# A decoder step whose second MLP block returns to eight products, with a chain for the final squares and later sums and loads

## The chip, the core and the metric

One core of one Trainium2 chip runs the whole step in one launch. The metric is device time in microseconds, the median of the runs shown.

## What is computed

One decoder layer over a prompt of 2048 tokens and a sample of 8 x 4 tokens: a mixer (state-space and retention groups in parallel), attention over 256 memory tokens, an MLP with squared ReLU, and a final norm. The change lies in the MLP and the norm behind it:

```
h = rmsnorm(x, p['g_mlp'])
x = x + jnp.square(jax.nn.relu(h @ p['w_up'])) @ p['w_down']
...
y_prompt = rmsnorm(xp, g_final)
y_sample = rmsnorm(xs, g_final)
```

with a model width of 1024 (eight tiles of 128 features, `KT`) and a hidden width of 4096.

## The kernel before

Features lie on the partitions, tokens in the columns. The prompt is cut into four blocks of 512 tokens, `blk[0]` to `blk[3]`. After the mixer, each block goes through the output projection (`out_items`), attention, and the MLP (`mlp_items`), one block after another. Block 1 carries the 32 sample tokens: their attention is done by 48 small "sample units" (`sample_items`), each with a 512 KB weight of its own, which are put between the units of block 1's MLP; their columns then join block 2, whose MLP works on 544 columns in two pieces of 272.

Numbers are fp32, and the products get their accuracy from splits: a tile is written as a high part (ACT, rounded to the matmul's format) and a low part (the rest, by DVE or POOL), and a product is three matmuls (`PASSES`). So each weight unit of 128 x 1024 numbers is loaded into `raw` (three buffers), split into `whl` (three buffers), and used by PE. The loader works a few units ahead. All loads and stores of this part are issued from one queue, SP, in order: one that waits holds up those behind it.

The MLP runs in eight groups `g` of 512 hidden features. The order is up(0), up(1), down(0), up(2), down(1), ..., up(7), down(6), down(7).

- **Direct down** (`down_items`, block 0): four units of 24 matmuls of 512 columns; each output tile is added to `x` by DVE. PSUM tiles are called `dn`, and the hidden operands `actl`.
- **Seven products** (`up_seven`, `hidden`, `down_seven`, `seven`; blocks 1 to 3): the weight, the hidden tensor and the result are cut in quarters, and seven products of half the columns take the place of eight (`JOBS`). POOL squares the ReLU into `hc`, forms sums and differences of quarters, and each of seven operands is split into `actl`. PSUM tiles are called `m` here; each of the 14 jobs of a group ends with two half-width additions into `x` on DVE. Seven units of weights per group.
- The weight's own sums and differences of quarters (`sums`) are made once, by a side program that starts with block 0: it loads half of `w_s[n]` into `wsum`, POOL makes four operations, and the result is stored to `s_d`; 32 halves in all. `seven_src` reads `w_s` or `s_d`.

The instructions of every engine are put in order when the program is built. `Order` follows a model of the engines' times; side programs (generators) are resumed when the model's clock passes their wake time, and a `yield` of a number, or of a key of the table `SET`, adds that many nanoseconds before the next step. So `SET["ws1"]` and `SET["ws2"]` say how far apart the steps of `sums` stand. `cat_load` is the side program that loads the next block's eight mixer tiles (`cat_d`) and splits them into `act`; it starts, with six loads of the next block's `xT`, when up(7) is done. `squares` makes the sum of squares (`acc`) for a norm: ACT squares a tile into a `relu` buffer (two of them), POOL or DVE adds it. In `seven` it was called in the last group, right behind the last job of each half.

Line 200 is the helper that records every operation of DVE, ACT, POOL and SP, and line 454 the one for matmuls; so tiles, not lines, tell instructions apart.

Of the kernel before, what the change touches and what calls it, by code (L numbers as in the profile page):

```python
# [13 lines left out]
AF = mybir.ActivationFunctionType  # L14
ALU = mybir.AluOpType
# [3 lines left out]
P = 128  # L19
# [7 lines left out]
SB = 1  # L27
TM_ = BT + NS
KT = D // P
# [30 lines left out]
    "l_ds": 4, "x_hs": 2, "x_hq": 2, "x_hl": 2, "q_h": 250, "ws": 700, "ws1": 1500, "ws2": 5000}  # L60


class Item:
# [268 lines left out]
def tile_decoder_step(ctx: ExitStack, tc: tile.TileContext, ins: dict, outs: dict):  # L332
    nc = tc.nc
    model = Model()
    V, A, G, SY = (Engine(model, e, k) for e, k in ((nc.vector, "V"), (nc.scalar, "A"), (nc.gpsimd, "G"), (nc.sync, "SP")))
    T = nc.tensor

    def E(key):
        return Either(model, (V, G), key)
# [59 lines left out]
    def aux(name="ax"):  # L399
        return psum.tile([P, 512], F32, tag="ra", name=name, bufs=2)  # L400
# [7 lines left out]
    def xin():  # L408
        return com.tile([P, TM_], F32, tag="x", name="x", bufs=3)

    def act():
        return com.tile([P, 2, TM_], F32R, tag="act", name="act", bufs=NA)
# [29 lines left out]
    od = Order(model, load_unit, split_unit)  # L442
# [27 lines left out]
    def split(dst, src, scale=None):  # L470

        split_first(dst, src, scale)
        split_rest(dst, src, scale)
# [405 lines left out]
    def pt(name, shape, tag, bufs=1, dt=F32):  # L879
        return pool[name].tile(list(shape), dt, tag=tag, name=tag, bufs=bufs)  # L880

    def call(f):
        return Item(f)
# [145 lines left out]
    def shared_acc():  # L1029
        return com.tile([P, TM_], F32, tag="acc", name="acc")  # L1030
# [673 lines left out]
    def rk(shape, tag, bufs=1, dt=F32):  # L1704
        return pt("rest", shape, tag, bufs, dt)
# [4 lines left out]
    def squares(B, o, t, lo=0):  # L1710
        x, c = B["x"][o], slice(lo, t)
        if o == 0:
            if lo == 0:
                B["acc"] = shared_acc()
            A.activation(B["acc"][:, c], x[:, c], AF.Square)
        elif lo:
            if o > 1:
                V.tensor_tensor(out=B["acc"][:, c], in0=B["acc"][:, c], in1=B["sq"][:, c], op=ALU.add)
            B["sq"] = rk((P, TM_), "relu", 2)
            A.activation(B["sq"][:, c], x[:, c], AF.Square)  # L1720
        else:
            sq = rk((P, TM_), "relu", 2) if "rest" in pool else xin()
            A.activation(sq[:, c], x[:, c], AF.Square)
            (V if "tail" in B else E("x_rq")).tensor_tensor(out=B["acc"][:, c], in0=B["acc"][:, c], in1=sq[:, c], op=ALU.add)
# [27 lines left out]
    def cat_load(B):  # L1752
        t, c0 = B["t"], B["c0"]
        B["cats"], cs = [], []

        def dma():
            ci = xin()
            SY.dma_start(ci[:, :t], cat_d[len(cs), :, c0:c0 + t])
            cs.append(ci)
        dma()  # L1760
        dma()
        for k in range(KT):
            if k == NA - 4 and B["b"] == 0:
                while "hold" in M:
                    yield 500
            yield [cs[k]]
            if k + 2 < KT:
                dma()
            a = act()
            split(a[:, :, :t], cs[k][:, :t])  # L1770
            B["cats"].append(a)
# [339 lines left out]
    def mlp_items(B, nxt):  # L2111
        t = B["tm"]
# [117 lines left out]
        def seven(g, u, name, st):  # L2230
            h = t // 2

            def job(w):
                v = w.rearrange("p s (k m c) -> p s k m c", k=2, m=2)
                while name not in a_of[g]:
                    od.resume(hid[g])
                for m in range(2):
                    if name in ("A11", "S1"):
                        st[name, m] = (aux2 if name == "S1" and not held["zps"] else dense)("m7")
                    ps = st["S1" if name in ("S1", "S4") else "A11", m] if name != "A12" else aux("m7")  # L2240
                    for k in range(2):
                        for i, (a, b) in enumerate(PASSES):
                            mm(ps[:, :h], v[:, a, k, m, :], a_of[g][name][:, k, b, :h],
                               start=(name in ("A11", "A12", "S1") and k + i == 0), stop=(k == 1 and i == 2), skip_group_check=True)
                        yield
                    o = 4 * u + m + (2 if name in ("A22", "S1", "S3") else 0)
                    lo = h if name in ("S2", "S4", "S1", "S3") else 0
                    V.tensor_tensor(out=B["x"][o][:, lo:lo + h], in0=ps[:, :h], in1=B["x"][o][:, lo:lo + h], op=ALU.add)
                    if name == "A22" and g == 7:
                        if B["last"] and u:  # L2250
                            B["tail"] = True
                        squares(B, o - 2, t)
                        squares(B, o, t)
                B["prog"] = 14 * g + 7 * u + JOBS.index(name) + 1
            return job

        def down_seven(g):
            jobs = []
            for u in range(2):
                st = {}  # L2260
                for name in JOBS:
                    src = {"A11": ("w", 0), "A22": ("w", 1), "A12": ("w", 3), "S2": ("s", 0), "S1": ("s", 1),
                           "S3": ("s", 2), "S4": ("s", 3)}[name]
                    jobs.append((seven(g, u, name, st), src + (2 * g + u,)))
            for a, b in zip(jobs[0::2], jobs[1::2]):
                def fn(hl, a=a, b=b):
                    for i, j in enumerate((a, b)):
                        yield from j[0](hl[:, :, 512 * i:512 * i + 512])
                yield Item(fn, seven_src(a[1], b[1]), "v2", tag="l_ds")
            if g == 7:  # L2270
                yield call(lambda: B.__setitem__("fin", od.spawn(final(B, 0, t), B["acc"])))

        def mixed(items, part=1.0):
            for n, i in enumerate(items):
# [8 lines left out]
        count, smp = [0], sample_items()  # L2283
        yield call(lambda: B.__setitem__("ms", od.spawn(mlp_scale(), B["acc"])))
        hid = {}
        B["prog"] = 0
        use = [B["b"] > 0] * 8
        yield from (up_seven if use[0] else up_items)(0)
        yield Item(None, side=lambda: B["ms"])
        for g in range(8):  # L2290
# [44 lines left out]
    def final(B, lo, hi):  # L2335
        n, c, more, x = hi - lo, slice(lo, min(hi, BT)), hi > BT, B["x"]
        end = B["last"] and hi == BT
        cols = [(B["acc"][:, i:i + P], P) + ((B["sq"][:, i:i + P],) if lo else ())
                for i in range(lo, min(hi, BT), P)]
        if more:  # L2340
            cols.append((B["acc"][:, BT:hi], NS))
        if not end:
            yield SET["fi0"]
        rs = stats(pool["rest"], B["acc"], cols, "nf")
        if end:
            for o in (2, 5, 7):
                A.activation(x[o][:, lo:hi], x[o][:, lo:hi], AF.Copy, scale=g_fin[:, o:o + 1])
        else:
            yield "fi1"
        rf = rk((P, TM_), "rb")  # L2350
        ps = yield from spread(rf, rs, n, 4, rk((P, TM_), "sq") if n >= BT else None)
        if not end:
            yield "fi2"
        for i, o in enumerate((0, 2, 1, 3, 5, 4, 6, 7) if end else range(KT)):
            xo = x[o][:, lo:hi]
            if end:
                if o in (2, 5, 7):
                    G.tensor_tensor(out=xo, in0=xo, in1=rf[:, :n], op=ALU.mult)
                else:
                    V.scalar_tensor_tensor(out=xo, in0=xo, scalar=g_fin[:, o:o + 1], in1=ps[:, :n],  # L2360
                                           op0=ALU.mult, op1=ALU.mult)
            elif o % 3 == 2 or B["last"] and o % 3 == 1:
                A.activation(xo, xo, AF.Copy, scale=g_fin[:, o:o + 1])
                G.tensor_tensor(out=xo, in0=xo, in1=rf[:, :n], op=ALU.mult)
            else:
                V.scalar_tensor_tensor(out=xo, in0=xo, scalar=g_fin[:, o:o + 1], in1=rf[:, :n],
                                       op0=ALU.mult, op1=ALU.mult)
            (A if end and i % 2 else SY).dma_start(outs["yT"][o, :, B["b"] * BT + lo:B["b"] * BT + c.stop], x[o][:, c])
            if more:
                SY.dma_start(outs["yT"][o, :, SEQ:], x[o][:, BT:hi])  # L2370
            if not end:
                yield 900 if B["last"] else 700
# [152 lines left out]
```

## Time and profile before

| | |
|---|---|
| median of 3 runs | 3103.31 us (3101.45 to 3104.01) |
| profiled execution, its own time | 3108.91 us |
| its span | 3107.1 us |
| mean granted TensorE clock | 0.977 |
| MLP of block 0 (direct), about | 1081 to 1442 us |
| MLP of block 1 (seven products and the sample) | 1595.24 to 2049.83 us |
| MLP of block 2 (seven products, 544 columns) | 2197 to 2586.2 us |
| MLP of block 3 (seven products) | 2735.4 to 3088.5 us |
| HBM traffic | 388.69 MB read, 54.17 MB written |

Times are microseconds from the start of the span. "A <- B" in a wait says that A waited and B's end released it; a busy share is that of the stretch named. The span is the time between the first and the last instruction; a little of an execution lies outside.

### The profile page before, as it was taken

What the parts mean: (1) busy time and instruction counts of PE and PEld (TensorE: products, weight loads), DVE (VectorE), ACT (ScalarE), POOL (GpSimd) and SP (SyncE); (2) the same over time, 40 slices, a digit from 0 to 9 for tenths busy, and PEclk for the clock granted to TensorE, in tenths of its full rate; (3) what the DMA queues carried; (4) which work ended last, traced back from release to release, by engine and by line L of the source; (5) the groups of instructions that cost most, each with busy time, mean ns of one, the idle gap of its engine ahead of it and who ended that gap; (6) DMA issues with size and microseconds to landing.
All of it is one profiled execution on the core that took longest, in us unless ns stands there. A gap on an engine that the chain in (4) does not pass through costs nothing. (4 is left out here: it accounts for less than half of the span.)

```text
span 3107.1 us, 47076 instructions
## 1 busy us (share of the span) xinstructions
PE 2926.4 (94%) x17530; PEld 2585.1 (83%) x17530; DVE 2137.3 (69%) x3818; ACT 1118.1 (36%) x1570; POOL 1676.6 (54%) x1813
## 2 busy tenths in 40 slices
PE   8898899999989999999998999899999999999997
PEld 6788788877978878888977888778899988878887
DVE  8968868778765644435467888755676676577777
ACT  4432232322453422223334443443333334333333
POOL 6534434253655566556646665552565566266664
PEclk9999999999999999999999999999999999999998
DMA  5463352433784445455435555652244354224443
GB/s 149 135 175 103 104 150 96 150 130 98 250 267 143 136 149 168 149 183 180 144 108 156 171 169 161 198 163 89 82 130 123 123 159 149 89 90 135 136 138 113
DMA packets 195429, 445.94 MB, mean 144 GB/s; under 512 B 21856, under 2 KB 73728, under 8 KB 195200
## 3 DMA queue, kind: packets, MB, share of 16 engines
q1 hardware_dynamic: 194624, 441.89, 45.0%
q8 instruction: 138, 2.26, 0.3%
q10 hardware_dynamic: 576, 1.05, 0.1%
q14 instruction: 91, 0.75, 0.1%
HBM read 388.69 MB, written 54.17 MB: 143 GB/s over the span
## 5 line engine op out<-in xcount | busy, mean ns | idle before, releaser
L200 ACT ACTIVATE whl<-raw 128x1024 fp32r<-128x1024 f32 (+1 forms) x578 | 603.3, 1050 | 942.9 <-PE dn L454 478.6
L454 PE MATMUL dn<-act,whl 128*128 128x512 f32 (+2 forms) x4704 | 926.6, 351 | 8.1 <-DVE relu L200 2.7
L200 DVE TENSOR_TENSOR whl<-raw,whl 128x512 fp32r<-128x512 f32 (+1 forms) x717 | 760.2, 1091 | 169.9 <-ACT whl L200 162.2
L454 PEld LDWEIGHTS dn<-act,whl 128*128 128x128 f32 x4704 | 760.9, 192 | 119.5 <-issue 6.0
L454 PE MATMUL m<-actl,whl 128*128 128x256 f32 (+1 forms) x4032 | 527.5, 290 | 49.8 <-DVE x L200 44.4
L454 PEld LDWEIGHTS m<-actl,whl 128*128 128x128 f32 x4032 | 506.8, 192 | 69.2 <-DVE x L200 44.9
L200 POOL TENSOR_TENSOR whl<-raw,whl 128x256 fp32r<-128x256 f32 x500 | 396.9, 825 | 183.4 <-ACT whl L200 177.9
L454 PE MATMUL dn<-z,whl 128*128 128x512 f32 (+1 forms) x2160 | 436.0, 353 | 0.0
L454 PEld LDWEIGHTS dn<-z,whl 128*128 128x128 f32 x2160 | 354.0, 189 | 56.5 <-issue 0.9
L454 PE MATMUL dn<-actl,whl 128*128 128x512 f32 x1536 | 360.6, 393 | 4.1 <-DVE x L200 4.1
L200 POOL TENSOR_TENSOR actl<-hc,actl 128x256 fp32r<-128x256 f32 (+1 forms) x288 | 274.1, 981 | 144.9 <-ACT actl L200 144.2
L454 PEld LDWEIGHTS dn<-actl,whl 128*128 128x128 f32 x1536 | 286.6, 188 | 69.6 <-DVE x L200 5.5
L200 POOL TENSOR_TENSOR hc<-relu 128x256 f32<-128x256 f32 (+1 forms) x192 | 160.3, 855 | 261.3 <-DVE relu L200 259.7
L200 DVE SCALAR_TENSOR_TENSOR relu<-dn,rb 128x512 f32<-128x512 f32 (+1 forms) x160 | 91.5, 588 | 284.3 <-PE dn L454 221.5
L200 DVE TENSOR_TENSOR x<-dn,x 128x512 f32<-128x512 f32 (+1 forms) x232 | 151.8, 669 | 173.2 <-PE dn L454 172.6
L200 DVE TENSOR_TENSOR x<-m,x 128x256 f32<-128x256 f32 (+1 forms) x672 | 249.7, 417 | 16.2 <-PE m L454 14.7
L454 PE MATMUL dn<-whl,act 128*128 128x512 f32 x768 | 200.5, 409 | 11.8 <-ACT whl L200 7.0
L200 POOL TENSOR_TENSOR acc<-acc,relu 128x512 f32<-128x512 f32 (+1 forms) x73 | 110.5, 1514 | 170.0 <-ACT relu L200 166.1
L454 PEld LDWEIGHTS dn<-whl,act 128*128 128x128 f32 x768 | 166.4, 254 | 35.4 <-ACT whl L200 7.7
L200 POOL TENSOR_TENSOR wsum<-wsum 128x256 f32<-128x256 f32 x128 | 114.6, 895 | 52.5 <-DMA wsum<-in_w_s 46.1
L200 ACT ACTIVATE actl<-hc 128x512 fp32r<-128x512 f32 (+1 forms) x144 | 87.1, 626 | 39.3 <-POOL hc L200 39.3
L454 PE MATMUL sc<-whl,act 128*128 128x256 f32 x576 | 81.3, 293 | 14.9 <-ACT p L200 10.3
(326 smaller groups left out, 3265.9 us busy)
## 6 DMA issues: line engine op xcount, KB each, us to landing
raw<-in_w_up SPq DMA_DIRECT2D x128, 512.0 KB, 3.7
raw<-s_d SPq DMA_DIRECT2D x72, 512.0 KB, 3.7
raw<-in_w_s SPq DMA_DIRECT2D x96, 256.0 KB, 3.6
raw<-in_w_out SPq DMA_DIRECT2D x32, 512.0 KB, 4.0
raw<-wq_d SPq DMA_DIRECT2D x32, 512.0 KB, 3.7
wsum<-in_w_s SPq DMA_DIRECT2D x32, 512.0 KB, 4.1
raw<-wo_d SPq DMA_DIRECT2D x32, 512.0 KB, 4.2
s_d<-wsum SPq DMA_DIRECT2D x32, 512.0 KB, 3.4
```

The lines of the kernel that those rows point to most:

```text
L200: return f(*args, **kw)
L454: T.matmul(out, lhsT, rhs, start=start, stop=stop, **kw)
```

## The change

Block 1 uses the direct down product (`use` is true for blocks above `SB`, which is 1). The final squares of blocks 2 and 3 become a side program, `squares_chain`, that is fed by a list and joined before the final norm. `sums` waits longer between its steps. `cat_load` waits 1500 ns more before each split, for block 3 alone.

```
-    "l_ds": 4, "x_hs": 2, "x_hq": 2, "x_hl": 2, "q_h": 250, "ws": 700, "ws1": 1500, "ws2": 5000}
+    "l_ds": 4, "x_hs": 2, "x_hq": 2, "x_hl": 2, "q_h": 250, "ws": 700, "ws1": 3000, "ws2": 12000, "cl0": 1500, "sq0": 300}
...
             yield [cs[k]]
+            if B["b"] > SB + 1:
+                yield SET["cl0"]
             if k + 2 < KT:
                 dma()
...
                     if name == "A22" and g == 7:
-                        if B["last"] and u:
-                            B["tail"] = True
-                        squares(B, o - 2, t)
-                        squares(B, o, t)
+                        B["sqs"].extend((o - 2, o))
+                        if o == 2:
+                            B["acc"] = shared_acc()
+                            B["ssq"] = od.spawn(squares_chain(B))
...
+        def squares_chain(B):
+            for k in range(KT):
+                while len(B["sqs"]) <= k:
+                    yield 300
+                x = B["x"][B["sqs"][k]]
+                yield [x]
+                if k == 0:
+                    A.activation(B["acc"][:, :t], x[:, :t], AF.Square)
+                    continue
+                sq = rk((P, TM_), "relu", 2)
+                A.activation(sq[:, :t], x[:, :t], AF.Square)
+                yield [sq, B["acc"]]
+                (V if B["last"] and k > 3 else G).tensor_tensor(out=B["acc"][:, :t], in0=B["acc"][:, :t], in1=sq[:, :t], op=ALU.add)
+                yield SET["sq0"]
...
-                yield call(lambda: B.__setitem__("fin", od.spawn(final(B, 0, t), B["acc"])))
+                def fin():
+                    od.join(B["ssq"])
+                    B["fin"] = od.spawn(final(B, 0, t), B["acc"])
+                yield call(fin)
...
-        B["prog"] = 0
-        use = [B["b"] > 0] * 8
+        B["prog"], B["sqs"] = 0, []
+        use = [B["b"] > SB] * 8
```

On PE, in the second group of block 1's MLP (`zps` is the sample units' PSUM tile, `pq` a transpose of the sample's queries), this stood before:

```order
L454 MATMUL zps<-whl,pmk 64x512 x4
L454 MATMUL m_14755<-actl,whl 128x256 x6
L454 MATMUL m_14766<-actl,whl 128x256 x6
L454 MATMUL m_14774<-actl,whl 128x256 x6
L454 MATMUL m_14786<-actl,whl 128x256 x3
L458 MATMUL pq<-ident,s_14759 128x32 x4
L454 MATMUL m_14786<-actl,whl 128x256 x3
```

And with the change, at the same place and, behind it, at the third head's step from scores (`pp` transposes them) to values:

```order
L454 MATMUL zps<-whl,pmk 64x512 x4
L454 MATMUL dn<-actl,whl 128x512 x18
L458 MATMUL pq<-ident,s_14683 128x32 x4
L454 MATMUL dn<-actl,whl 128x512 x6
L454 MATMUL zps<-whl,pmk 64x512 x4
...
L458 MATMUL pp<-ident,s_16214 128x32 x2
L454 MATMUL dn<-z,whl 128x512 x12
L454 MATMUL zps<-whl,pmk 64x256 x8
```

Wide matmuls of the direct product stand where pairs of half-width ones stood, and between `pp` and the first unit that reads `pmk` there are twelve of them.

On SP, among the weight loads of block 1's MLP, there was nothing of the sums before (the last store had been issued ahead of it):

```order
L200 DMA raw<-in_w_up 128x1024 x3
L200 DMA raw<-in_cK 128x1024
L200 DMA raw<-in_w_up 128x1024
L200 DMA raw<-in_cK 128x1024
L200 DMA raw<-in_w_s 128x2x512
L200 DMA raw<-s_d 128x1024
```

With the change, a load and a store of the sums stand between the sample's units (`cK`, `cV`) and those of the product:

```order
L200 DMA raw<-in_w_down 128x1024
L200 DMA raw<-in_cK 128x1024
L200 DMA s_d<-wsum 512x1x256
L200 DMA raw<-in_w_down 128x1024
L200 DMA raw<-in_cK 128x1024
L200 DMA raw<-in_w_down 128x1024 x2
L200 DMA wsum<-in_w_s 128x4x256
L200 DMA raw<-in_cV 128x1024
L200 DMA raw<-in_w_up 128x1024
L200 DMA raw<-in_cV 128x1024
L200 DMA s_d<-wsum 512x1x256
```

The quarters of block 1's own weights have gone from the queue, and 12 of the 32 stores to `s_d` have come into this stretch.

On SP, at the end of block 2, where block 3's tiles are loaded, this stood before:

```order
L200 DMA raw<-in_w_s 128x2x512
L200 DMA raw<-s_d 128x1024 x2
L200 DMA x<-in_xT 128x512 x6
L200 DMA x<-cat_d 128x512 x5
L200 DMA raw<-in_w_s 128x512 x3
L200 DMA raw<-s_d 128x512
L200 DMA x<-cat_d 128x512 x2
```

And with the change:

```order
L200 DMA raw<-in_w_s 128x2x512
L200 DMA raw<-s_d 128x1024 x2
L200 DMA x<-in_xT 128x512 x6
L200 DMA x<-cat_d 128x512 x2
L200 DMA raw<-in_w_s 128x512 x2
L200 DMA x<-cat_d 128x512
L200 DMA raw<-in_w_s 128x512
L200 DMA raw<-s_d 128x512
L200 DMA x<-cat_d 128x512 x2
```

The five tile loads that stood in a row now let weight loads through between them. Of the eight residues (`act<-x,act`) of these tiles, seven are on DVE with the change and four were before; the others are on POOL.

## Rows read from the trace of the kernel before

**Rows 1.** The page: busy us, share of the span and instructions of each engine.

```profile
PE 2926.4 (94%) x17530; PEld 2585.1 (83%) x17530; DVE 2137.3 (69%) x3818; ACT 1118.1 (36%) x1570; POOL 1676.6 (54%) x1813
```

**Rows 2.** Busy time by stretches: length, busy us (count) of each engine, clock, DMA share, GB/s.

```profile
core 0: us, PE busy (x) PEld busy (x) DVE busy (x) ACT busy (x) POOL busy (x), PEclk, DMA share, GB/s
...
1155.15:1397.93 242.78, 242.78 (x1057) 198.12 (x1056) 97.11 (x109) 58.67 (x67) 146.12 (x169) 1.00 0.52 167
1595.24:2049.83 454.59, 410.26 (x2475) 357.18 (x2473) 350.93 (x549) 191.28 (x242) 266.40 (x273) 0.96 0.54 165
1737.65:1763.07 25.42, 25.42 (x125) 20.78 (x124) 16.96 (x20) 8.06 (x10) 14.86 (x15) 1.00 0.54 167
2298.32:2320.60 22.28, 21.75 (x171) 21.19 (x169) 21.44 (x42) 9.65 (x11) 15.25 (x16) 1.00 0.43 133
2530.38:2586.21 55.83, 47.55 (x339) 45.56 (x337) 49.65 (x86) 24.18 (x32) 35.81 (x34) 0.91 0.55 162
...
3045.34:3088.46 43.12, 41.27 (x337) 40.04 (x335) 41.07 (x81) 18.99 (x24) 27.56 (x27) 1.00 0.38 118
```

**Rows 3.** Waits of PE from 1595 to 2050 us (total, times, longest).

```profile
PE m L454 <- DVE x L200: 28.7, 19, 7.4
PE zps L454 <- DVE whl L200: 3.5, 1, 3.5
PE zps L454 <- ACT whl L200: 3.4, 1, 3.4
...
PE zps L454 <- POOL pmk L200: 1.4, 1, 1.4
...
PE pq L458 <- DVE s L200: 1.0, 2, 0.7
```

**Rows 4.** Timeline of ACT in block 1 (start, us, operation, idle before).

```profile
1632.22 1.67 ACT L200 ACTIVATE actl<-hc 128x512 fp32r<-128x512 f32 x3 [4.39 <-POOL hc L200]
1633.80 2.93 ACT L200 ACTIVATE whl<-raw 128x1024 fp32r<-128x1024 f32 x3
```

**Rows 5.** Timeline of PE: half a direct group in block 0, a seven-product group in block 3.

```profile
1199.27 2.91 PE L454 MATMUL dn<-act,whl 128*128 128x512 f32 x12
...
1221.43 22.14 PE L454 MATMUL dn<-actl,whl 128*128 128x512 f32 x96
...
2850.23 2.92 PE L454 MATMUL dn<-act,whl 128*128 128x512 f32 x12
...
2893.47 2.92 PE L454 MATMUL dn<-act,whl 128*128 128x512 f32 x12
```

**Rows 6.** Timeline of PE in block 1: a sample unit, and a step from scores to values.

```profile
1705.24 1.10 PE L454 MATMUL zps<-whl,qm 128*64 128x256 f32 x8
1706.17 5.83 PE L454 MATMUL m<-actl,whl 128*128 128x256 f32 x48
...
1797.29 0.31 PE L458 MATMUL pp<-ident,s 32*128 32x32 f32 x2
1797.53 3.04 PE L454 MATMUL dn<-z,whl 128*128 128x512 f32 x12
...
1802.18 0.93 PE L454 MATMUL zps<-whl,pmk 128*64 128x256 f32 x6 [1.38 <-POOL pmk L200]
```

**Rows 7.** Timeline of SP's queue at the end of block 2.

```profile
2519.03 14.59 SPq L200 DMA_DIRECT2D x<-cat_d  x5
2533.68 1.37 SPq L200 DMA_DIRECT2D raw<-in_w_s  x3
```

**Rows 8.** Waits of SP's queue in block 0, from 1155 to 1397 us.

```profile
SPq L200 <- POOL wsum L200: 73.7, 14, 8.1
```

**Rows 9.** The instructions that write `wsum` on POOL (ns min, median, max; first and last start).

```profile
L200 POOL TENSOR_TENSOR wsum<-wsum x128: 722/740/1794, 998.4 to 1562.5; 128x256 f32<-128x256 f32 x128
```

**Rows 10.** Timelines of DVE and of PE at the end of block 3.

```profile
3091.21 0.69 DVE L200 TENSOR_TENSOR acc<-acc,relu 128x512 f32<-128x512 f32 x1 [0.46 <-ACT relu L200]
...
3091.96 1.87 PE L454 MATMUL st<-ones,acc 128*128 128x2 f32 x8 [3.33 <-DVE acc L200]
```

## The prediction

> **What bounds the kernel now.** I read the page first. TensorE (PE) is busy for 94% of the span and no other engine passes 69% [rows 1], so over the whole program PE is what the others must keep fed. That is an average, so the next view was the busy time by stretches. Two MLP stretches tell nearly everything. In block 0, which computes the down product directly, PE is busy for 242.78 of 242.78 us at clock 1.00, while the sums of quarters run beside it [rows 2]. In block 1, which uses seven products and also carries the sample units, PE is busy for 410.26 of 454.59 us at a granted clock of 0.96 [rows 2]. Third, the waits of PE in that stretch: 28.7 us stand before seven-product matmuls (`m`) that wait for DVE's addition into `x`, 19 times, the longest 7.4; 6.9 us in one place where a sample unit waits for its split weights; and only small waits that are the sample's own: 1.4 for `pmk`, 1.0 for `pq` [rows 3]. Fourth, the timeline of ACT at that 6.9 us place: ACT stood 4.39 us behind POOL's `hc`, did three `actl` pieces, and only then split the weights [rows 4]. So even this wait comes from the quarters of the hidden tensor that seven products need.
>
> How much is lost there? A direct group (four up units and four down units, 24 wide matmuls each) costs 242.78/5.5 = 44.14 us, since that stretch holds five and a half groups [rows 2]. A seven-product group that runs smoothly, in block 3, takes 2893.47 - 2850.23 = 43.24 us, of which the up half is 22.16 us (1199.27 to 1221.43) and the seven products 21.08 [rows 5]. A sample unit takes 0.93 us (1705.24 to 1706.17), and a small transpose of the sample some 0.31 [rows 6]. Block 1 before therefore holds 8 x 43.24 + 48 x 0.93 + 12 x 0.31 = 394.2 us of PE work, and takes 454.6: 60.4 us are lost to waits and to the lower clock after them.
>
> **Part 1: block 1 goes back to direct products.** PE gets 8 x (44.14 - 43.24) = 7.2 us more work, so its floor is 8 x 44.14 + 44.6 + 3.7 = 401.4 us. What goes is the whole machinery: the quarter sums and splits of the hidden tensor on POOL and ACT, 224 half-width additions into `x` on DVE (64 full-width ones take their place), and 24 weight units of the 56. What stays beside the direct product are the sample units. Is that density bearable? From 1737.65 to 1763.07 the old kernel runs four up units with four sample units between them, and PE is busy for 25.42 of 25.42 us at 167 GB/s [rows 2]; direct down units have the same size and pace as up units. Block 0 shows that direct down units with the sums beside them run without a gap. I add the sample's own waits: after the transpose `pp`, PE has twelve or eighteen wide matmuls before it wants `pmk` (the order shows this in all four heads), and the one place of before with twelve waited 1.38 us for POOL's `pmk` [rows 6]. Four times 1.4 and the 1.0 of `pq` are 6.6 us. The stage comes to 408.0, a gain of **46.6 us**. The bounds: no wait at all (401.4, a gain of 53.2), and a cost of the moved sums, next.
>
> **Part 2: the sums later.** The 128 POOL operations of the sums ran from 998 to 1562 us, 32 halves in 564 us or 17.6 us each [rows 9]. The new delays add about 10 us to a half (two of 1.5 us, one of 7), so some 28 us each: about 880 us, ending near 1880, inside block 1; the order puts the last store about two thirds through block 1's loads, well ahead of block 2's first use. Twelve of the 32 stores now stand on SP's queue among block 1's weight loads. A store waits for POOL, and everything behind it on SP waits too: from 1155 to 1397 SP waited 73.7 us for `wsum`, 14 times, the longest 8.1 [rows 8], and PE lost nothing [rows 2]. I cost it at nothing: the cover is the load's lead of a few units. In block 1 a load is wanted every 3.2 us in place of 5.5, so this cover is thinner; were it gone, twelve stores would cost up to 12 x 8.1 = 97 us. I take zero because the later first sum and the later store (1.5 us each) make precisely these waits shorter, and keep a part of the price in the range.
>
> **Part 3: the loads for block 3 later.** At the end of block 2 two down products stand back to back. They take 55.83 us where twice an undisturbed one is 2 x 22.28 = 44.56 [rows 2], a loss of 11.3. SP shows why: five issues of `x<-cat_d` held its queue from 2519.03 for 14.59 us, and the next quarter weights went out at 2533.68 [rows 7]; DVE then came late with everything. In the new order two `cat_d` loads go first and the others by ones and twos between weight loads, after 1.5 us more each. Block 3, with the same two downs and no loads to make, loses 43.12 - 2 x 21.08 = 1.0 us [rows 2], so at most 10.3 can come back. But DVE is busy for 21.44 of 22.28 us in an undisturbed down of this block [rows 2], and seven of the eight residues of the loaded tiles now stand on DVE, four before. I take **6.3 us** (5 stay); the bounds are 0 and 10.3.
>
> **Part 4: squares as a chain.** In blocks 2 and 3 the same eight squares and seven additions are issued, only elsewhere. Nothing waits for them before the last product is done, so the cover is the down product itself; without it the cost is at the end: the statistics matmul `st` starts at 3091.96, behind the last addition to `acc`, which starts at 3091.21 [rows 10]. The new order moves one addition of four from before `x`'s last addition to behind it; the chain ACT, DVE, PE is as long. Zero, between -1 and +1.
>
> **A rule that speaks against this.** The rows of part 1 say: PE's added work counts 7.2 us, its removed waits 53.8. The Trainium skill, page Perfetto Trace Analysis, section Identifying the Most-Contended Engine, says to find the engine of highest occupancy and to optimize that one first; here this is PE, and the change gives it more to do. By that rule alone the sum would be +7.2 us; by the rows of the stretch it is -46.6. The same page allows that the contended engine changes between regimes, and the trace agrees: 0.96 and 44.3 idle us in block 1, none in block 0.
>
> **Sum.** 46.6 + 6.3 = 52.9 us off the profiled execution's own 3108.9 us is 3056.0. That execution lies 5.6 us above the median of the runs shown (3103.3); the median should fall to **3050 us**.
>
> **Rivals.**
> - *The end of block 2 stays as it is* (seven residues on a full DVE). 3108.9 - 46.6 - 5.6 = 3056.7. For it: 21.44 of 22.28. Against: the 14.59 us hold on SP is gone. 14%.
> - *All clean*: 401.4 in block 1 and 10.3 at the end of block 2, 3039.8. For it: block 0's gapless rows. Against: the `pmk` distances. 12%.
> - *The stores cost a part*: 2 us of each of twelve reach PE, 24 us: 3074. 9%.
> - *Slower, by SP's queue*: each store holds the loads for its longest wait, 8.1 us, none of it covered. Block 1 becomes 408 + 97 = 505, the kernel 3108.9 + 50.4 - 6.3 - 5.6 = 3147. It is slower than before once a store costs PE more than (46.6 + 6.3)/12 = 4.4 us. For it: twelve stores among loads that come nearly twice as often. Against: 14 such waits cost block 0 nothing. 2%.
> - *The waits are not those of seven products*: the sample units cause them, they stay, and only PE's 7.2 us count: 3110.5. Against: 28.7 of the 44 idle us stand before `m` and name DVE's `x`. 2%. (The rule of the Trainium skill's page named above would give this time.)
>
> **How the numbers follow.** The forecast has 61%. The range 3040 to 3067 holds it with the first two rivals, 87%, less what lies at their edges and in the 2 us spread of the runs. A measurement here tells about 0.2% (6 us) from no change. Faster: 61 + 14 + 12 + 9 = 96%. The last rival lies just at the bound, half on each side: same 1%, slower 3%.
>
> **What would show it.** Right: in block 1's MLP PE's stretch is 402 to 412 us at clock 0.99 or more, with no `m` in it; PE's waits there are a few of 1 to 2 us before `zps` and small transposes; the pair of downs that closes block 2 takes about 50 us. Wrong: PE waiting in block 1 for `whl` behind ACT waiting for DMA, with SP waiting for `wsum` ahead of it; sums still running when block 2's first down starts; or 55 us and more for the two downs.

## The result, and the profile after

The changed kernel takes **3069.9 us** (median of four runs, 3066.8 to 3077.3) where the old one takes 3103.7 on the same chip: a ratio of 0.9895, with an interval of 0.9874 to 0.9916. The forecast was 3050, with a range of 3040 to 3067. The direction was right, the size was not: 34 us came where 53 were expected. The profiled execution took 3066.77 us, its span is 3064.8.

The page of the changed kernel, busy us, share of the span and instructions of each engine (before: [rows 1]):

```profile
PE 2920.2 (95%) x16954; PEld 2550.3 (83%) x16954; DVE 2025.5 (66%) x3548; ACT 1080.1 (35%) x1522; POOL 1593.8 (52%) x1737
```

The two stretches the prediction speaks of, by stretches (length, busy us and count of each engine, clock, DMA share, GB/s): block 1's MLP, and the pair of downs that closes block 2.

```profile
1594.96:2012.49 417.53, 412.12 (x1900) 329.49 (x1898) 235.11 (x281) 153.95 (x195) 230.63 (x240) 0.99 0.54 177
2491.40:2544.76 53.36, 45.76 (x339) 44.06 (x338) 51.21 (x89) 25.83 (x35) 30.79 (x31) 0.97 0.52 154
```

Against [rows 2], block 1 went from 454.59 to 417.53 us, 37.1 less (46.6 expected), and the pair from 55.83 to 53.36, 2.5 less (6.3 expected). All else in the span moved by 2.8 us together. The waits of PE in block 1's MLP (total, times, longest), to be held against [rows 3]:

```profile
PE sp L458 <- DVE parts L200: 3.3, 1, 3.3
PE op L458 <- DVE s L200: 0.6, 1, 0.6
PE pq L458 <- DVE s L200: 0.6, 1, 0.6
PE dn L454 <- DVE whl L200: 0.5, 1, 0.5
PE dn L454 <- ACT whl L200: 0.5, 1, 0.5
```

The 28.7 us before `m` are gone, and so is every wait for `pmk`, of which four were expected. A new one stands on top: PE waits for `parts`, the last step of the norm's chain on DVE. On the timeline of DVE there (start, us, operation, what it idled for):

```profile
1601.50 0.16 DVE L200 TENSOR_SCALAR ms<-st 128x4 f32<-128x4 f32 x1 [0.72 <-PE st L454]
1601.70 0.52 DVE L200 TENSOR_SCALAR rsy<-ms 128x4 int32<-128x4 int32 x1
1602.25 0.16 DVE L200 TENSOR_TENSOR rst<-rsy 128x4 f32<-128x4 f32 x1
1602.45 0.59 DVE L200 SCALAR_TENSOR_TENSOR rst<-rst,ms 128x4 f32<-128x4 f32 x1
1603.07 0.66 DVE L200 SCALAR_TENSOR_TENSOR rsy<-rst,rsy 128x4 f32<-128x4 f32 x1
1603.77 0.65 DVE L200 TENSOR_TENSOR rst<-rsy 128x4 f32<-128x4 f32 x1
...
1606.69 0.16 DVE L200 TENSOR_TENSOR parts<-rsy,parts 128x4 fp32r<-128x4 f32 x1
```

Seven of the eleven operations on 128 x 4 numbers take 0.52 to 0.66 us, six of them one after the other. In the old kernel the same chain, with POOL idle, had 0.15 to 0.17 us throughout, as here (timeline of DVE, before):

```profile
1603.13 0.16 DVE L200 SCALAR_TENSOR_TENSOR rst<-rst,ms 128x4 f32<-128x4 f32 x1
1603.32 0.16 DVE L200 SCALAR_TENSOR_TENSOR rsy<-rst,rsy 128x4 f32<-128x4 f32 x1
```

What POOL does meanwhile in the changed kernel (timeline of POOL):

```profile
1599.66 3.36 POOL L200 TENSOR_TENSOR wsum<-wsum 128x256 f32<-128x256 f32 x3
1602.98 2.77 POOL L200 TENSOR_TENSOR whl<-raw,whl 128x256 fp32r<-128x256 f32 x4
1605.71 0.72 POOL L200 TENSOR_TENSOR wsum<-wsum 128x256 f32<-128x256 f32 x1
```

and, taken apart, the second and third of the three at its start:

```profile
1601.45 0.74 POOL L200 TENSOR_TENSOR wsum<-wsum 128x256 f32<-128x256 f32 x1
1602.27 0.75 POOL L200 TENSOR_TENSOR wsum<-wsum 128x256 f32<-128x256 f32 x1
```

Each slow operation of DVE lasts about as long as one of POOL's (2.77/4 = 0.69), and each ends 0.02 to 0.03 us behind the end of one. The short one at 1602.25 began in the pause between two of POOL's (1602.19 to 1602.27), and `ms<-st`, which reads PSUM, was short beside POOL too. The others become short again when POOL stops at 1606.43. So the suspicion after this reading: the sums of quarters, which the change moved into block 1, stand, with a weight split of POOL's between them, beside the one short chain that PE waits for.

At the end of block 2 SP's queue did become free, as the order said (timeline of SP's queue, to be held against [rows 7]):

```profile
2480.09 1.02 SPq L200 DMA_DIRECT2D x<-cat_d  x2
2482.45 0.81 SPq L200 DMA_DIRECT2D raw<-in_w_s  x2
2483.30 0.43 SPq L200 DMA_DIRECT2D x<-cat_d  x1
```

and the pair hardly shortened. DVE, by operation and shape in the pair (count, busy us, mean ns, idle before):

```profile
L200 DVE TENSOR_TENSOR whl<-raw,whl 128x512 fp32r<-128x512 f32 x24 | 23.9, 1035 | 0.0
L200 DVE TENSOR_TENSOR x<-m,x 128x272 f32<-128x272 f32 x55 | 21.5, 430 | 1.9 <-PE m L454 1.7
L200 DVE TENSOR_TENSOR act<-x,act 128x512 fp32r<-128x512 f32 x7 | 6.7, 964 | 0.0
```

Seven residues of block 3's tiles take 6.7 us of an engine that is busy for 51.21 of 53.36 us.

### The profile page after: what moved, and what is told of

The parts are those of the page before. It is cut to its first block, busy times and chain, and to the rows that moved or that the text cites. A ratio compares the mean times of both kernels' runs of the same rounds, so it can differ in the third digit from the quotient of the medians.

```text
span 3064.8 us, 45220 instructions
## 1 busy us (share of the span) xinstructions
PE 2920.2 (95%) x16954; PEld 2550.3 (83%) x16954; DVE 2025.5 (66%) x3548; ACT 1080.1 (35%) x1522; POOL 1593.8 (52%) x1737
## 5 line engine op out<-in xcount | busy, mean ns | idle before, releaser
L200 DVE TENSOR_TENSOR whl<-raw,whl 128x512 fp32r<-128x512 f32 (+1 forms) x571 | 647.6, 1161 | 183.7 <-ACT whl L200 175.5
L200 POOL TENSOR_TENSOR whl<-raw,whl 128x256 fp32r<-128x256 f32 x636 | 503.3, 822 | 241.6 <-ACT whl L200 235.0
L454 PE MATMUL dn<-actl,whl 128*128 128x512 f32 x2304 | 545.2, 394 | 3.9 <-DVE x L200 2.9
L454 PEld LDWEIGHTS dn<-actl,whl 128*128 128x128 f32 x2304 | 429.0, 188 | 102.4 <-DVE x L200 3.7
L454 PE MATMUL m<-actl,whl 128*128 128x272 f32 (+1 forms) x2688 | 343.7, 287 | 18.1 <-DVE x L200 17.1
L454 PEld LDWEIGHTS m<-actl,whl 128*128 128x128 f32 x2688 | 332.9, 189 | 28.6 <-DVE x L200 24.6
L200 POOL TENSOR_TENSOR actl<-hc,actl 128x272 fp32r<-128x272 f32 (+1 forms) x192 | 178.9, 961 | 84.0 <-ACT actl L200 83.7
L200 POOL TENSOR_TENSOR hc<-relu 128x272 f32<-128x272 f32 (+1 forms) x128 | 98.8, 792 | 177.9 <-DVE relu L200 176.8
L200 POOL TENSOR_TENSOR actl<-sq,actl 128x512 fp32r<-128x512 f32 x64 | 85.5, 1336 | 201.7 <-DVE sq L200 194.4
L200 DVE TENSOR_TENSOR x<-m,x 128x272 f32<-128x272 f32 (+1 forms) x448 | 167.9, 421 | 11.2 <-PE m L454 10.4
```

Of the source, the lines that this page charges most:

```text
L200: return f(*args, **kw)
L454: T.matmul(out, lhsT, rhs, start=start, stop=stop, **kw)
```

## The experiments

Twelve runs, each compared with the old kernel on its own chip (its median was 3103.7 us for the changed kernel, 3107.0 for a1 and e1 to e3, 3111.1 for e5 to e9, 3103.4 for e10 to e13; so ratios, not medians, compare across these groups). "Block 1" is the time from the start of its MLP norm's statistics (`st`) to the first `st` of block 2 on PE, so it takes in some work on both sides of the MLP; "pair" is the pair of downs that closes block 2.

| run | median us | ratio (interval) | block 1 | pair |
|---|---|---|---|---|
| the old kernel | 3103.7 | 1 | 502.4 | 55.83 |
| the changed kernel | 3069.9 | 0.9895 (0.9874 to 0.9916) | 465.4 | 53.36 |
| a1_again | 3076.4 | 0.9902 (0.9883 to 0.9922) | 465.8 | 54.65 |
| e1_direct_only | 3063.2 | 0.9860 (0.9837 to 0.9884) | 457.2 | 54.01 |
| e2_sums_early | 3063.3 | 0.9856 (0.9837 to 0.9875) | 458.1 | 53.28 |
| e3_seven_kept | 3106.7 | 1.0000 (0.9986 to 1.0014) | 498.3 | 53.31 |
| e5_one_half_held | 3061.6 | 0.9844 (0.9829 to 0.9858) | 456.8 | 53.31 |
| e7_tiles_on_pool | 3063.6 | 0.9854 (0.9831 to 0.9877) | 457.2 | 57.47 |
| e8_half_on_pool | 3061.9 | 0.9842 (0.9815 to 0.9868) | 456.8 | 53.70 |
| e9_quiet_norms | 3066.3 | 0.9851 (0.9828 to 0.9873) | 457.0 | 53.35 |
| e10_no_residue | 3060.3 | 0.9856 (0.9834 to 0.9879) | 457.2 | 45.30 |
| e11_tiles_early | 3056.1 | 0.9846 (0.9826 to 0.9866) | 456.8 | 46.82 |
| e12_loads_unpaced | 3065.8 | 0.9870 (0.9847 to 0.9893) | 456.8 | 53.25 |
| e13_both_held | 3051.8 | 0.9831 (0.9811 to 0.9851) | 457.8 | 46.80 |

### The changed kernel again (a1_again)

> The changed kernel again, unaltered. Theory: its time is 3070 us within 3, block 1's MLP takes 417.5 us within 1 in the profiled run, the wait for `parts` 3.3 us. Rival: the runs' spread of 10 us (3066.8 to 3077.3) lies in block 1, and this profile shows another length there, with other waits.

Block 1 and the wait (3.2 us) came out the same; the total did not (3076.4). Between these two profiles the difference lies in neither of the places that the change touches. PE's timeline at the first `st` of block 0's attention shows where, first the changed kernel, then this run of it:

```profile
990.69 0.95 PE L454 MATMUL st<-ones,acc 128*128 128x2 f32 x8
```

```profile
1001.23 0.95 PE L454 MATMUL st<-ones,acc 128*128 128x2 f32 x8
```

The same instructions reach this point 10.5 us later; from there to the end the two spans take 2074.1 and 2078.1 us. Over the fourteen profiles that point lies between 986.7 and 1001.2, and between 990.4 and 1001.2 in the four of one chip (a1, e1 to e3). The mixer, ahead of everything that was changed, gives 10.5 of the 14.5 us between the two spans, and places must be compared, not totals, where a few us matter.

### One part at a time (e1, e2, e3)

Only block 1's product in the old kernel:

```
-        use = [B["b"] > 0] * 8
+        use = [B["b"] > SB] * 8
```

> The old kernel with one edit: block 1's MLP uses the direct down product; sums, loads and squares as before. Theory A (the sums that run on POOL inside block 1 slow DVE's short operations in block 1's norm chain): here all sums are done before block 1, so DVE's 128x4 operations take about 0.2 us as in the old kernel, the wait of PE for the norm's `parts` is 0.2 us in place of 3.3, the low clock behind it goes too (4.5 us), and block 1's MLP takes about 410 us in place of 417.5; the pair of downs at the end of block 2 stays at 55.8. Kernel: 3103.7 - 44.6 = 3059. Rival B (the sums in block 1 cost nothing; the stage was simply counted too short): block 1 takes 417, kernel 3103.7 - 37 = 3067.

Only the sums' waits of the changed kernel put back:

```
-"ws1": 3000, "ws2": 12000
+"ws1": 1500, "ws2": 5000
```

> The changed kernel with the two waits of the sums put back to 1.5 and 5 us, so that they end before block 1. Theory A (sums in block 1 slow its norm chain): block 1's MLP falls from 417.5 to about 410, kernel 3070 - 7.5 = 3062. Rival B (sums cost nothing there): 417, kernel 3070. Rival C (the later sums were worth their move, because early ones hold SP's queue or POOL in block 0): block 0 grows and the kernel is at 3070 or above although block 1 is shorter.

Both of these put back in the changed kernel, so that only the tile loads and the squares remain changed:

```
-        use = [B["b"] > SB] * 8
+        use = [B["b"] > 0] * 8
...
-"ws1": 3000, "ws2": 12000
+"ws1": 1500, "ws2": 5000
```

> The changed kernel with seven products in block 1 again and the sums' waits as in the old one: only the later tile loads and the chain of squares remain of the change. Theory D (DVE is full at the end of block 2, so later loads free SP and bring little): the pair of downs takes about 53.4 us (55.8 before), the tail about 1 us less, block 1 as in the old kernel (454.6); kernel 3103.7 - 3.7 = 3100. Rival (the term of the prediction, 6.3 us, shows when nothing else is changed): pair 49.5, kernel 3097. Rival (the gain of 2.5 us belonged to the run): pair 55.8, kernel 3104.

Part 1 alone shortens block 1 by 45.3 us (502.4 to 457.2), more than the whole change does (37.1). Taking the later sums back gives 7.3 us of block 1 (465.4 to 458.1). Theory A forecast 7.5; rivals B and C fall. One of its figures missed: the wait for `parts` in e1 and e2 is 1.3 us, not 0.2, since a weight split of POOL's still meets the chain there. The squares and the later loads alone give nothing that the medians can tell (1.0000); in the profile of that run block 1 was 4.2 us and the pair 2.5 us shorter than in the old kernel's, and the median shows neither. Since each kernel's places come from one profile, the 45.3 and 37.1 us may hold some 4 us that belong to the old kernel's profile.

### One half of the sums held (e5)

```
                 yield SET["ws1"]
+                if n == 10 and h.start:
+                    yield 14000
```

> The changed kernel with one edit: the one half of the sums that POOL works on during block 1's norm chain starts 14 us later; the eleven halves behind it stay in block 1. Theory A (POOL's operations slow DVE's 128x4 operations, and that alone is what the sums cost): the wait for `parts` falls from 3.3 to about 1.3 us (POOL's split of a weight unit still overlaps two of the operations), the matmuls behind it run at their normal pace, and block 1, from its norm's `st` to block 2's first `st`, takes about 459 us in place of 465.4: as much as with all sums moved out (458.1). Rival E (it is the number of sums beside the product, through SP or POOL, that costs): at most 1 us comes back, 464 to 465.

Block 1 takes 456.8 us with the held half and the ten behind it (not eleven) still in it. So their number costs nothing, and to hold the one half that met the norm's chain gives the whole 8.6 us back. By stretches, the beginning of block 1's MLP to `parts`, and the next 30 matmuls; the changed kernel, then this one:

```profile
1594.96:1606.91 11.95, 8.69 (x42) 6.91 (x41) 10.79 (x16) 5.14 (x7) 11.16 (x11) 1.00 0.17 56
1606.91:1616.95 10.04, 10.04 (x30) 7.26 (x30) 4.58 (x6) 2.81 (x4) 3.44 (x3) 0.66 0.46 154
```

```profile
1593.46:1603.40 9.94, 8.68 (x42) 6.90 (x41) 8.76 (x16) 5.13 (x7) 8.33 (x7) 1.00 0.22 68
1603.40:1610.38 6.98, 6.98 (x30) 5.29 (x31) 4.13 (x6) 2.12 (x4) 2.15 (x1) 1.00 0.24 79
```

The wait costs 2.0 us, and the granted clock of 0.66 behind it (between the levels of 1.2 and 2.4 GHz, after PE had stood still for 3.3 us; behind the wait of 1.3 us it is 1.00) another 3.1. These 5.1 us are traced to the chain. The other 3.5 are four small waits of the changed kernel (2.1), three of them some 50 us later, and slower matmuls (1.4). They stand in a1 too and are gone here; whether the half beside the chain makes them, or the order that the program takes with it, was not traced. This kernel has one wait in block 1, and it is the rest of the same thing:

```profile
PE sp L458 <- DVE parts L200: 1.3, 1, 1.3
```

POOL still splits a weight unit until 1601.95, and all operations of the chain that overlap it are slow but `ms<-st`; those behind it are short (timelines of POOL and of DVE):

```profile
1598.15 3.80 POOL L200 TENSOR_TENSOR whl<-raw,whl 128x256 fp32r<-128x256 f32 x4
```

```profile
1600.61 0.66 DVE L200 TENSOR_TENSOR rst<-rsy 128x4 f32<-128x4 f32 x1
1601.30 0.66 DVE L200 SCALAR_TENSOR_TENSOR rst<-rst,ms 128x4 f32<-128x4 f32 x1
1602.00 0.16 DVE L200 SCALAR_TENSOR_TENSOR rsy<-rst,rsy 128x4 f32<-128x4 f32 x1
1602.19 0.16 DVE L200 TENSOR_TENSOR rst<-rsy 128x4 f32<-128x4 f32 x1
```

The Trainium skill, page SBUF — State Buffer, section SBUF: two separate sides, says that VectorE and GpSimd share one pair of ports by an exclusive lock, taken for a whole instruction, where a VectorE operation has two inputs in SBUF (and GpSimd reads SBUF) or runs in one of its two-port modes. The trace agrees: DVE's 0.16 us become 0.66, and each slow operation ends just behind one of POOL's. `rsy<-ms`, with one input, took 0.52 us in the changed kernel too; the trace does not show in which mode it ran.

### POOL kept idle in both norms (e9), and a second half held (e13)

e9 has the early sums of e2 and these edits:

```
+                if n == 2 and h.start:
+                    yield 14000
...
-    eng=ve("e_up1" if m % 2 else "e_up")
+    eng=V if g == 0 and m == 2 else ve("e_up1" if m % 2 else "e_up")
```

> The changed kernel with the sums early, with POOL kept idle during the norm chains of blocks 0 and 1: one half of the sums starts 14 us later in block 0, and one weight split of each block (the third unit of its first group) goes from POOL to DVE. Theory A: all of DVE's 128x4 operations take about 0.2 us; the wait for `parts` in block 0 falls from 2.9 us to under 0.5, that in block 1 from 1.3 to under 0.3; with the slow matmuls behind the longer one, block 0 gains about 5 us and block 1 about 1: kernel about 6 us below the one with early sums (3063). Rival (the short operations are slow for another reason): no change of the two waits; the added split on DVE makes them 1.2 us longer each.

All short operations took 0.16 or 0.17 us and both waits for `parts` are gone, so the cause of their length is settled. The gain is not what was forecast. Block 1 gained 1.0 (458.1 to 457.0). In block 0 the chain, from `st` to the first undisturbed twelve matmuls, takes 1097.13 - 1088.27 = 8.9 us where e2 takes 1098.67 - 1086.92 = 11.8: 2.9 of the 5 us. Ahead of it `st` waits for POOL's `acc`, as in e2:

```profile
PE st L454 <- POOL acc L200: 1.6, 1, 1.6
```

and the nine matmuls behind `st` took 3.9 us at a granted clock of 0.56, in place of 2.3 at 1.00; why the clock fell there behind the same wait and not in e2 is open. From block 0's `st` to block 1's, e9 is 0.5 us shorter than e2: 2.4 us were lost again between block 1's first `st` and this one, a stretch that ran from 97.6 to 101.2 us in the fourteen profiles. The ratio, 0.9851, shows no gain over e2's 0.9856.

e13 has the later sums, the tiles loaded early (e11, below), and a second half held:

```
-                if n == 10 and h.start:
+                if n in (1, 10) and h.start:
```

> The kernel with the tiles of block 3 loaded early, and with a second half of the sums held for 14 us, the one that POOL works on in block 0's norm chain. Theory A: in block 0 the wait for `parts` falls from 3.3 to about 1.3 us and the matmuls behind it keep their pace: from block 0's `st` to block 1's, 514.7 falls to about 509 us; block 1 stays at 457. Kernel: 5 us below the run with the tiles early alone. Rival: block 0's chain waits for another thing next (ACT's `rb` or the `acc` of POOL), and under 2 us come back, as in the run with quiet norms (0.5).

The wait in block 0 fell from 3.24 to 1.25 us, with no wait for `acc` ahead of it, and from `st` to the first undisturbed twelve matmuls the chain takes 1090.19 - 1081.62 = 8.6 us where e11 takes 1097.66 - 1085.74 = 11.9. So 3.3 us are shown, not 5: the whole stretch from block 0's `st` to block 1's did fall from 514.4 to 509.9, but it lay at 511.1 and 509.9 in e7 and e8 as well, whose block 0 is that of e2 (514.5).

### The pair at the end of block 2 (e7, e8, e10, e11, e12)

The two lines of `cat_load` taken out, on e5:

```
-            if B["b"] > SB + 1:
-                yield SET["cl0"]
```

> The changed kernel with one half of the sums held, and without the two lines that put the tile loads of block 3 later: the five issues of tiles stand in a row on SP again. Theory D: SP is held for some 14 us as before, and the pair takes 53 to 54 us all the same; the later loads were worth under 1 us. Rival (the term of the prediction): without them the pair goes back to 55.8 us or more, block 2 takes 2.5 us or more longer.

SP is held as it was before (timeline of SP's queue), and the pair takes the same 53.25 us (by stretches):

```profile
2474.92 14.57 SPq L200 DMA_DIRECT2D x<-cat_d  x5
2489.54 1.37 SPq L200 DMA_DIRECT2D raw<-in_w_s  x3
```

```profile
2486.24:2539.49 53.25, 46.44 (x338) 44.41 (x337) 49.33 (x86) 24.17 (x32) 36.05 (x34) 0.94 0.55 170
```

So part 3, taken whole, is worth nothing. But the hold was not harmless: two things cancel. In the old order (e12, and the old kernel) DVE does four of the residues and stands idle for ACT's `act`; in the new order it does seven and stands for none. First DVE, by operation and shape in the pair (count, busy us, mean ns, idle before), in e12 and in the old kernel, then ACT on its timeline in e12:

```profile
L200 DVE TENSOR_TENSOR act<-x,act 128x512 fp32r<-128x512 f32 x4 | 3.9, 1016 | 2.0 <-ACT act L200 2.0
L200 DVE TENSOR_TENSOR act<-x,act 128x512 fp32r<-128x512 f32 x4 | 3.9, 1017 | 2.8 <-ACT act L200 2.8
```

```profile
2494.88 1.06 ACT L200 ACTIVATE whl<-raw 128x1024 fp32r<-128x1024 f32 x1 [6.78 <-DMA raw<-in_w_s]
```

ACT stood 6.78 us for the weights that SP sent behind the tiles, and DVE stood 2.0 us for the `act` that ACT made after them. The later loads save DVE these 2.0 us and give it three more residues, 6.7 - 3.9 = 2.8 us. e1, with SP held for 14.58 us, agrees with 54.01; the old kernel's 55.83 is the longest of the three profiles with that order, and the changed kernel itself had 54.65 in its second profile.

Is it DVE? With the residues left out and a copy by ACT in their place:

```
+            if B["b"] > SB + 1:
+                A.activation(a[:, 1, :t], cs[k][:, :t], AF.Copy)
+            else:
                 split_rest(a[:, :, :t], cs[k][:, :t])
```

> The changed kernel with one half of the sums held (as in that run), and with the residues of block 3's eight tiles left out: ACT writes a copy of the tile in their place (0.6 us each, ACT is busy for half of the time), so DVE has 6.7 us less work in the pair of downs that closes block 2, POOL has no more, and the tile buffers come free early. Theory D (DVE's work sets the pair): 53.3 - 6.7 = 46.6 us, near twice an undisturbed down (44.6). Rival G (loads and SP's queue set it): 52 to 53 us. Rival H (the relu wait and the order of additions set it): 50 to 53.

```profile
2481.51:2526.81 45.30, 43.51 (x339) 42.41 (x337) 43.58 (x82) 30.01 (x43) 29.01 (x30) 1.00 0.57 182
```

DVE's 51.2 us became 43.6, and the pair 45.3, near the 44.6 of two undisturbed downs. This run also frees the tile buffers early; that loads do not set e5's pair is read from DVE, which waits there for nothing but PE (3.1 us at its start, 1.5 behind). So DVE's work sets it. The median does not show the 8 us (ratio 0.9856 for e5's 0.9844); block 2, from its norm's `st` to block 3's first, does, with 428.1 for 435.9. Can the work go elsewhere? Not to POOL, in the kernel with early sums (e2):

```
+                G.tensor_tensor(out=a[:, 1, :t], in0=cs[k][:, :t], in1=a[:, 0, :t].bitcast(F32), op=ALU.subtract)
```

> The changed kernel with the sums early (as in the run before), and all eight residues of block 3's tiles on POOL; in the changed kernel seven are on DVE (6.7 us of DVE's time in the pair of downs that closes block 2). Theory D (DVE's work sets that pair; it waits for almost nothing there): the pair falls from 53.3 by the 6.7 us of the seven residues to about 47 us, kernel about 6 us below the one with early sums (3063). Rival F (POOL's operations slow DVE as they did in the norm, so the time is only moved): pair 51 to 54. Rival G (the loads or SP set it): 53.3.

and with every second one there (`if B["b"] > SB + 1 and k % 2`):

> As the run with all eight residues on POOL, but with every second one there, the others on DVE or POOL as before. Theory D: about half of the gain, pair near 50 us. Rival F: 51 to 54. Rival G: 53.3.

Theory D was wrong here: 57.47 and 53.70. With all eight on POOL, DVE is busy for only 46.2 us, but other things are late (stretch; PE's wait in it; SP's queue and ACT on their timelines):

```profile
2486.07:2543.54 57.47, 48.46 (x339) 46.65 (x337) 46.23 (x82) 25.81 (x35) 40.04 (x38) 0.91 0.46 143
```

```profile
PE m L454 <- POOL actl L200: 3.0, 1, 3.0
```

```profile
2489.29 8.37 SPq L200 DMA_DIRECT2D x<-cat_d  x2
2497.72 0.42 SPq L200 DMA_DIRECT2D raw<-s_d  x1
```

```profile
2502.26 1.06 ACT L200 ACTIVATE whl<-raw 128x1024 fp32r<-128x1024 f32 x1 [8.36 <-DMA raw<-s_d]
```

POOL frees the tile buffers late, so SP stands 8.37 us at two tile loads and ACT 8.36 us for the weights behind them; and POOL's own `actl` is late by 3.0. The first is rival G; rival F, as it was put, is not shown by it. With every second one there, DVE did four residues and 48.87 us of work, but stood 3.7 us for ACT (2.2 for `whl`, 1.5 for `act`). To another time, then:

```
+            early = g == 6 and nxt is not None and nxt["b"] > SB + 1
+            if early:
+                def first():
+                    M["hold"] = True
+                    nxt["cl"] = od.spawn(cat_load(nxt))
+                yield call(first)
             if g < 7:
...
-            if k == NA - 4 and B["b"] == 0:
+            if k == NA - 4 and B["b"] != 1:
```

(`hold`, which keeps back the last two tiles, is taken away behind up(7).)

> The changed kernel with one half of the sums held, and the loads of block 3's tiles started at the beginning of up(7), where DVE is busy for 12.5 of 25 us, the last two tiles after it. All the work is done, only elsewhere. Theory D: up(7) stays at 24.1 us, the pair falls to about 47 us, and block 2, from its norm's `st` to block 3's first `st`, from 435.9 to about 430; kernel about 6 us below the run with one half held. Rival F (DVE and POOL slow each other, so the residues cost the same wherever they stand): up(7) takes 2 to 4 us longer, and the pair falls as much as under D; net 2 to 4. Rival G: the earlier loads delay weights, pair 53 or more.

The stretches of up(7) and of the pair:

```profile
2459.80:2483.91 24.11, 24.11 (x195) 24.11 (x193) 17.04 (x23) 9.13 (x13) 13.79 (x15) 1.00 0.72 244
2483.91:2530.73 46.82, 44.08 (x339) 42.50 (x337) 45.26 (x83) 22.53 (x29) 32.53 (x31) 1.00 0.48 149
```

The up half takes no longer with six residues in it, since DVE was idle there for half of the time, and the pair loses 6.5 us; block 2, from its norm's `st` to block 3's first, fell from 435.9 to 429.3. The ratio, 0.9846, does not show it against e5's 0.9844 from another chip; against e12 on the same chip the median is 9.8 us lower, with intervals that overlap. e13, which has both repairs, is the fastest kernel of the study: 3051.8 us, 0.9831 of the old one. Its interval overlaps that of e11, so the step between these two rests on the chain above and not on the medians.

## Why the prediction was right or wrong

- **Part 1, right, by two errors that cancel.** "The stage comes to 408.0": with no sums in its norm, e5's block 1 MLP takes 1593.46 to 2002.36, 408.9 us. But the 6.6 us of sample waits in that sum never came (the one wait is 1.3), and PE's floor was not 401.4 but 407.6 (its busy time there). The wide matmuls between sample units are slower than block 0's: a direct unit takes 5.60 us (1752.91 to 1758.51 in e5) where 44.14/8 = 5.52 was taken, and the 64 units together 358.3 for 353.1, 5.2 us more. The norm's `st` and `sp` (some 1.3) were not counted.
- **Part 2, the step that failed.** "I cost it at nothing: the cover is the load's lead." It looked at SP, and SP was indeed harmless: its waits for `wsum` in block 1's MLP came to 12.4 us, the longest 4.3; in e5 they came to 17.3, and PE waited there for `parts` alone. It ended where expected, too: the sums' last operation starts at 1902.1 (near 1880 was said). But POOL's operations were never placed beside DVE's. What the moved sums cost is 8.6 us of block 1 (465.4 to 456.8), all of which comes back when one half is kept from a chain of eleven short operations; 5.1 us are traced to that chain. It is not that sums in block 1 are dear; this schedule put one in the wrong 7 us. Without this cost the medians are 3063.3 (e2) and 3061.6 (e5), inside the range of 3040 to 3067.
- **Part 3, a term that came to nothing.** "SP shows why": the hold of 14.59 us [rows 7] was real, but it cost DVE some 2 us (2.0 in e12, 2.8 before) and not 6.3, and the new order spends them on three more residues (2.8). The doubt that the text raised itself, DVE's 21.44 of 22.28 us and seven residues, was the cause, and the first rival, at 14%, was the right one. 6.3 us were taken; about 0 came (53.25 without the later loads, 53.31 with them).
- **Part 4, right**: nothing. `st` waits 2.93 us for `acc` in the tail, 3.33 before [rows 10].
- **The conversion.** The profiled execution of before lay 5.6 us above its median, that of after 3.1 below. Taking the 5.6 off was taking off chance: 8.7 of the 19.9 us by which the median was missed. The rest is block 1 (417.5 for 408.0, 9.5), the pair (3.8), and -2.1 elsewhere, in which 0.4 is the rounding of 3050.4 to 3050. The old kernel's profile may have been long in the very places that were priced (e3's is 4.2 and 2.5 us shorter there); then part of the 5.6 was counted twice, once in the gains and once here. One profile of each does not show it.
- What stays open: by the places the two profiles of the changed kernel gain 41 and 37 us behind the first 1000, by the medians 34 and 31. The intervals of the medians reach to 39 and 36. The old kernel's one profile may be long behind that point: e3's is 8.8 us shorter there, at a ratio of 1.0000. One profile of the old kernel does not settle it.

## What to carry to other kernels

Before work is moved on POOL, lay its new place beside DVE's short serial chains, since there each DVE operation can cost a whole POOL operation; holding back the one piece that meets the chain keeps the rest of the move. A queue that stands still costs what the engine behind it starves: look how long the consumer was idle, and for what, before pricing the hold (here 2 us of a hold of 14.6). Here work on a full engine was best moved to a time when that engine is idle, not to another engine.

## What was not expected of the hardware

- DVE's operations on 128 x 4 numbers took 0.16 us alone and 0.38 to 0.75 beside POOL; each slow one ended 0.02 to 0.03 us behind a POOL operation. Splits of 128 x 512 in the pair averaged 1.04 us, and two took 1.29 together in e7 at 2503.35, where POOL was idle.
- The same instructions of the first 990 us varied by 14.5 us over fourteen profiles.
